# Filler products in parts with fixed places, and attention heads as a pipeline of groups, in a two-layer hybrid decoder step on one core

## The chip, the cores and the metric

The program runs on one core of one Trainium2 chip. The time is the device time of one execution in microseconds (us). The kernel before was timed in three runs; the numbers of stages come from one further execution taken with a profile.

## The reference

One inference step of a decoder with two layers, for a prompt of 1024 tokens and for 8 sample tokens with a paged cache of 512 earlier positions each. The model width is 1024, the MLP width 4096, all in 32-bit floats.

```python
# layer 0                                   # layer 1
h = rmsnorm(x)                              h = rmsnorm(x)
a = diff_attention(h)   # 4 heads, T5 bias  a = forgetting_attention(h)  # 8 heads
b = hgrn2(h)            # 4 heads, scan     b = mlstm(h)                 # 4 heads, scan
x = x + concat(a, b) @ w_out                x = x + concat(a, b) @ w_out
x = x + relu(rmsnorm(x) @ w_up)**2 @ w_down # the same in layer 1, then a final rmsnorm
# differential attention, causal:
p = softmax(q1 @ k1.T / 8 + bias) - lam * softmax(q2 @ k2.T / 8 + bias)
# forgetting attention, causal, F the running sum of log forget values:
p = softmax(q @ k.T / 8 + F_q - F_k);  out = p @ v
```

New key and value rows, states and the normed outputs are returned.

## The kernel before

**Products.** A 32-bit product is computed as three products of values split into a high and a low part (`mm3`, L115): high by high, high by low, low by high. Weights come in blocks of 128 x 1024, loaded by SP's queue, rounded by ScalarE (L100) and subtracted by GpSimd (L101). The tokens are in two halves, u = 0 with 512 columns and u = 1 with 520, the latter as two blocks of 260 (`BLOCKS`). A unit of projection or of the MLP's up step is 24 products, a unit of the down step 12 (L121), each closed by VectorE.

**Heads.** In `diff_head` (L645) and `fox_head` (L1192) the queries of a half are four blocks of 128, taken as two groups g of two blocks. For each block: score products (`scores`, L557), the minimum on VectorE, the exponential on ScalarE (L587), the scaling (L669 and L670, or L1211 and L1213). Then, for each pair j of key blocks, the probabilities are transposed by TensorE (`prob_t`, L605), copied and split by ScalarE and VectorE (`split_t`, L593 and L594), and multiplied with the values (`pv`, L621). `pv` needs both halves of the split. A head's output goes through DRAM (`os`).

**Filler.** While the heads and the scans run, other work is given to TensorE by generators: `fill` holds projections of layer 0 and the halves of the MLP (`half`, L1303), `back` the sample work. `tick(n)` (L165) adds rate x n to a credit and takes one unit for each whole credit; a generator that says "wait" stops it. The heads tick after each score by L / 1024, L being the number of keys. `half` computes first the output projection of the scan's heads, then that of the attention heads, then an RMS (L240 to L254), then eight chunks of four up and eight down units. In layer 0 it says "wait" before its last down units, until the next stage has made room.

**Order.** The stages follow in `run` (L1440): gates and projections, first HGRN half (0.55 units per tick), first differential half (2.6), second differential half (1.5), second HGRN half with the layer's sample work (0.8); then for each u the rest of the filler, the odd projections, the forgetting half (5.0 for u = 0, 1.9 for u = 1), the mLSTM half (1.7, 1.0); at the end the last MLP half alone. The filler of u = 0 is the second half of layer 0's MLP, that of u = 1 the first half of layer 1's.

The order of the text isn't yet that of the engines' queues. The program is built with

```python
    with tile.TileContext(nc, schedule_with_timeline_sim=True) as tc:
```

so that a planner walks its own model of time and gives each engine the earliest instruction of the text that the model holds ready. An engine executes its queue in the order that results. Two accumulators in PSUM (`accM`) serve the filler.

## Time and profile before

| | us |
|---|---|
| median of three runs (2909.43 to 2916.26) | 2913.05 |
| the profiled execution | 2911.51 |
| its span, from the first to the last instruction | 2909.8 |
| mean granted TensorE clock | 0.961 of full speed |

The profile gives for each engine its busy time, and for each stretch of time the busy times, the number of instructions (x), the granted clock of TensorE as a share of 2.4 GHz, the busy share of the DMA engines and their rate. A product's recorded duration (0.28 us for 260 columns, 0.40 for 512) is longer than the distance at which products follow each other, since they overlap.

### The profile page before, as it was taken

The page shows a single profiled execution, that of the slowest core. Times are in us where ns is not written, and L with a number is a line of the kernel's source. Part 1 is how long each engine was busy: PE and PEld are TensorE (multiplying, and loading weights), DVE is VectorE, ACT ScalarE, POOL GpSimd, SP SyncE. Part 2 cuts the span into 40 slices and gives each one's busy share as a digit, 9 for nine tenths or more (in the row PEclk, how much of TensorE's full clock was granted, in tenths as well). Part 3 has the DMA queues.
Part 4 walks back from the last instruction along what each step waited for, and adds up shares of the span by engine and source line. Part 5 has one row for each costly group of instructions (what it writes and reads, how often), then busy time and mean ns, then how long its engine had stood idle before and what let it go on. Part 6 is the DMA issues. An engine that isn't in the chain of part 4 may idle for free. (4 is left out here: it accounts for less than half of the span.)

```text
span 2909.8 us, 44551 instructions
## 1 busy us (share of the span) xinstructions
PE 2772.4 (95%) x17408; PEld 2462.5 (85%) x17410; DVE 1357.5 (47%) x2668; ACT 1037.1 (36%) x1741; POOL 1147.6 (39%) x688
## 2 busy tenths in 40 slices
PE   8999997999999989989999989989999997999997
PEld 6999886888777768889999979978888875999997
DVE  5134468554456654374322255364444354522224
ACT  4111356454212312374332332154444331423233
POOL 3323323443338424432343435843433330344443
PEclk9999998999989979999999999999999995999998
DMA  4332544333436544533322254643322365322222
GB/s 143 113 121 81 157 143 130 103 93 105 146 87 193 170 146 146 163 89 107 123 87 91 92 156 152 226 126 95 93 91 79 98 173 156 95 89 94 94 88 74
DMA packets 174684, 349.72 MB, mean 120 GB/s; under 512 B 28914, under 2 KB 67298, under 8 KB 174474
## 3 DMA queue, kind: packets, MB, share of 16 engines
q1 hardware_dynamic: 174250, 346.81, 38.0%
q8 instruction: 137, 2.24, 0.3%
q0 software_dynamic: 224, 0.07, 0.2%
q14 instruction: 73, 0.60, 0.1%
HBM read 297.92 MB, written 48.88 MB: 119 GB/s over the span
## 5 line engine op out<-in xcount | busy, mean ns | idle before, releaser
L101 POOL TENSOR_TENSOR wl<-wr,wh 128x1024 fp32r<-128x1024 f32 (+1 forms) x361 | 870.2, 2411 | 1306.9 <-ACT wh L100 1221.3
L100 ACT ACTIVATE wh<-wr 128x1024 fp32r<-128x1024 f32 (+1 forms) x361 | 381.4, 1057 | 1038.9 <-PE acc L121 746.7
L121 PE MATMUL acc<-uh,wh 128*128 128x260 f32 (+1 forms) x2080 | 670.4, 326 | 33.1 <-DVE x L1324 15.6
L121 PE MATMUL acc<-ul,wh 128*128 128x260 f32 (+1 forms) x2080 | 663.8, 320 | 0.6 <-DVE ul L1292 0.3
L121 PE MATMUL acc<-xh,wh 128*128 128x260 f32 (+1 forms) x1760 | 588.6, 335 | 12.9 <-ACT xh L217 7.8
L121 PE MATMUL acc<-uh,wl 128*128 128x260 f32 (+1 forms) x1856 | 600.0, 324 | 0.0
L121 PE MATMUL acc<-xl,wh 128*128 128x260 f32 (+1 forms) x1760 | 585.9, 333 | 2.9 <-DVE xl L218 2.9
L121 PE MATMUL acc<-xh,wl 128*128 128x260 f32 (+1 forms) x1760 | 582.8, 331 | 0.0
L121 PEld LDWEIGHTS acc<-uh,wh 128*128 128x128 f32 x2080 | 393.7, 191 | 68.0 <-DVE x L1324 20.8
L121 PEld LDWEIGHTS acc<-ul,wh 128*128 128x128 f32 x2080 | 395.8, 190 | 29.9 <-DVE ul L1292 2.0
L1324 DVE TENSOR_TENSOR x<-acc,x 128x260 f32<-128x260 f32 (+1 forms) x464 | 237.4, 516 | 382.8 <-PE acc L121 382.0
L121 PEld LDWEIGHTS acc<-uh,wl 128*128 128x128 f32 x1856 | 352.7, 190 | 26.9 <-issue 0.2
L121 PEld LDWEIGHTS acc<-xh,wh 128*128 128x128 f32 x1760 | 332.6, 189 | 47.7 <-ACT xh L217 8.1
L121 PEld LDWEIGHTS acc<-xl,wh 128*128 128x128 f32 x1760 | 333.8, 190 | 32.3 <-DVE xl L218 3.9
L121 PEld LDWEIGHTS acc<-xh,wl 128*128 128x128 f32 x1760 | 333.3, 189 | 31.6 <-issue 1.3
L1298 DVE SCALAR_TENSOR_TENSOR acc<-acc,rb 128x260 f32<-128x260 f32 (+1 forms) x192 | 100.1, 523 | 236.8 <-PE acc L121 232.5
L121 PE MATMUL acc<-ih,wh 128*128 128x260 f32 (+2 forms) x600 | 192.3, 321 | 5.6 <-ACT wh L100 2.7
L121 PE MATMUL acc<-ih,wl 128*128 128x260 f32 (+2 forms) x600 | 190.5, 320 | 3.9 <-POOL wl L101 3.8
L121 PE MATMUL acc<-il,wh 128*128 128x260 f32 (+2 forms) x600 | 191.2, 319 | 0.0
L194 DVE TENSOR_TENSOR z<-acc,rb 128x512 f32<-128x512 f32 (+1 forms) x138 | 69.5, 510 | 249.5 <-PE acc L121 224.3
L1301 DVE TENSOR_TENSOR ul<-acc,uh 128x260 fp32r<-128x260 f32 (+1 forms) x192 | 98.5, 514 | 162.8 <-ACT uh L1300 162.3
L121 PE MATMUL acc<-x,wh 128*128 128x260 f32 x448 | 127.9, 288 | 0.8 <-DVE z L194 0.6
(406 smaller groups left out, 3884.1 us busy)
## 6 DMA issues: line engine op xcount, KB each, us to landing
wr<-in_w_up SPq DMA_DIRECT2D x128, 512.0 KB
wr<-in_w_down SPq DMA_DIRECT2D x128, 512.0 KB
wr<-in_w_in_o SPq DMA_DIRECT2D x48, 512.0 KB
wr<-in_w_out SPq DMA_DIRECT2D x32, 512.0 KB
wr<-in_w_in_e SPq DMA_DIRECT2D x27, 512.0 KB
qd<-qS SPq DMA_DIRECT2D x64, 128.0 KB
dk<-in_cache_k_a SPq DMA_DIRECT2D x32, 256.0 KB
dk<-in_cache_v_a SPq DMA_DIRECT2D x32, 256.0 KB
```

The source lines that it names most:

```text
L100: nc.scalar.activation(h[:, :kk, :m], r[:, :kk, :m], AF.Copy)
L101: nc.gpsimd.tensor_tensor(l[:, :kk, :m], r[:, :kk, :m], raw(h[:, :kk, :m]), op=ALU.subtract)
L121: nc.tensor.matmul(out, lhsT=w[:, k, :m], rhs=a[:, sl], start=(n == 0), stop=(n == last))
L194: nc.vector.tensor_tensor(d, p, r, op=ALU.mult)
L1298: nc.vector.scalar_tensor_tensor(p, p, 0.0, self.rb[u][:, sl], op0=ALU.max, op1=ALU.mult)
L1301: nc.vector.tensor_tensor(L[:, sl], p, raw(H[:, sl]), op=ALU.subtract)
L1324: nc.vector.tensor_tensor(x[f][:, sl], pt[:, :m], x[f][:, sl], op=ALU.add)
```

## The change

- `mm3_parts` splits a unit into parts of up to 4608 columns: a unit of 24 products of 512 columns becomes three parts of 8, one of 12 becomes two of 6. The generators give back a part's size in units of 4096 columns, and `tick` takes parts while the credit is above zero.
- While heads run (`self.chain`), the first product of each part is ordered behind the head product that was traced last (`self.after`): a score, a transpose or a `pv` product. The tie holds for TensorE's queue order.
- `attend` runs the heads as a pipeline of groups. In the first halves the scores stand two groups ahead, in the second halves one; loads stand up to one group further ahead. Between the transposes of a pair and its `pv` products come a tick and a share of the next group's score steps. Values are loaded and split a head ahead, and the heads' ends tick too.
- `pv` takes all terms of the high part before those of the low part.
- The rates are changed to parts. In the heads the rate is 1.

```diff
+    def mm3_parts(self, out, h, l, ah, al, ks, sl, m=128):
...
+        todo = [(w, a, k) for k in ks for w, a in ((h, ah[k]), (h, al[k]), (l, ah[k]))]
+        last = len(todo) - 1
+        per = -(-len(todo) // -(-len(todo) * cols // 4608))
+        for i in range(0, last + 1, per):
+            if i:
+                yield per * cols / 4096
+            for n in range(i, min(i + per, last + 1)):
+                w, a, k = todo[n]
+                with self.tc.issue_after(self.after) if self.chain and self.after and n == i else nullcontext():
+                    nc.tensor.matmul(out, lhsT=w[:, k, :m], rhs=a[:, sl], start=(n == 0), stop=(n == last))
+        return (last + 1 - i) * cols / 4096
...
-            while credit >= 1 and gens:
+            while credit > 0 and gens:
                 try:
-                    if next(gens[0]) == "wait":
+                    size = next(gens[0])
+                    if size == "wait":
+                        credit = 0.0
                         break
-                    credit -= 1
+                    credit -= size or 1
                 except StopIteration:
                     gens.pop(0)
...
-            nc.tensor.matmul(S[:, cs], lhsT=q2[:, qs], rhs=k2[:, cs], start=False, stop=True)
...
+
...
+        self.chain = True
+        N = len(groups)
+        for G in groups[:depth + lead]:
+            G.prep()
+        self.tick(4)
+        for G in groups[:depth]:
+            for step in G.steps:
+                step()
+                self.tick(0.7)
+        for n, G in enumerate(groups):
+            if n + depth + lead < N:
+                groups[n + depth + lead].prep()
+            nxt = groups[n + depth] if n + depth < N else None
+            todo = list(nxt.steps) if nxt else []
+            for j in range(G.pairs):
+                parts = G.tr(j)
+                share = 0 if nxt and nxt.late and j < G.pairs - 2 else -(-len(todo) // (G.pairs - j if not (nxt and nxt.late) else min(2, G.pairs - j)))
+                self.tick(max(gap - 0.4 * share, 0.4))
+                for _ in range(share):
+                    todo.pop(0)()
+                G.pv(j, parts)
+            G.end()
+        self.chain = False
...
                     n += 128
...
-            order = [(k0, t) for t in terms(k0)] + [(k1, t) for t in terms(k1)]
-        else:
-            t0 = terms(k0)
-            order = [(k0, t0[0])] + [(k1, t) for t in terms(k1)] + [(k0, t) for t in t0[1:]]
+        order = []
+        for x in range(2):
+            t0, t1 = ([(kb, t) for t in terms(kb) if t[1] == x] for kb in (k0, k1))
+            order += t0[:1] + t1 + t0[1:] if x == 0 else t1 + t0
         for n, (kb, (w, x)) in enumerate(order):
             half = kb == 2 * g + 1
...
+        def prep(h, g):
             if g == 2 * u:
...
+                if need:
+                    self.drain("fill", need[h])
+                parts[h] = self.diff_parts(h, u, hd)
+                if h == 0:
+                    vt[0] = self.values(self.O["va"][0:128, :], u, hd)
+
+        def score(h, i, m):
+            S = pS.tile([128, W], F32, name="S", tag="S")
+            L = self.scores(S, parts[h][m], i)
+            w = min(L, 256)
+            if m == 0:
+                st[h, i] = hd.tile([128, 2, 2], F32, name="st", tag="st", bufs=8)
+            es[m] = hd.tile([128, W], F32, name="e", tag="e", bufs=5 if u else 7)
+            self.soft_neg(S, L, es[m], st[h, i][:, m, :], self.bias[:, h, 256 - w:])
+            if m == 0:
...
+            P[h, i] = es[0]
+
+        def tr(h, g, j):
+            if h == j == 0 and g == 2 * u:
+                V[0] = self.diff_values(vt[0], u, hd, pm)
+            if g == 2 * u and j == 0:
+                po[h] = pm.tile([128, 512], F32, name="po", tag="po", bufs=1)
+                if h < 3 and not need:
+                    vt[h + 1] = self.values(self.O["va"][128 * h + 128:128 * h + 256, :], u, hd)
+            return self.prob_t(hd, pm, (P[h, 2 * g], P[h, 2 * g + 1]), g, j)
+
+        def pv(h, g, j, p):
+            Vh, Vl = V[h]
+            self.pv(po[h][:, 256 * (g % 2):256 * (g % 2) + 256], g, j, p, lambda kb: ((Vh[:, kb, :], 0), (Vh[:, kb, :], 1), (Vl[:, kb, :], 0)))
+
+        def end(h, g):
+            if g == 2 * u:
+                if h < 3:
+                    if need:
+                        vt[h + 1] = self.values(self.O["va"][128 * h + 128:128 * h + 256, :], u, hd)
+                    V[h + 1] = self.diff_values(vt[h + 1], u, hd, pm)
+                return
+            ot = hd.tile([128, 512], F32, name="ho", tag="ho", bufs=1)
+            self.head_norm(hd, po[h][:], pm, ot[:], self.lc[:, 6:7], None, 512, eps=self.lc[:, 4:5], thr=self.lc[:, 5:6])
+            nc.sync.dma_start(self.os[0][u][h][:, :512], ot[:])
+            self.tick(2.5 if u else 1.5)
+
+        groups = []
+        for h in range(4):
...
+                steps = [lambda h=h, i=i, m=m: score(h, i, m) for i in (2 * g, 2 * g + 1) for m in range(2)]
+                groups.append(Group(lambda h=h, g=g: prep(h, g), steps, g + 1, lambda j, h=h, g=g: tr(h, g, j),
+                                    lambda j, p, h=h, g=g: pv(h, g, j, p), lambda h=h, g=g: end(h, g), late=u == 1 and g == 2))
+        self.attend(groups, 1 if u else 2, 0 if u else 1, 1.3 if u else 1.0)
...
-                self.fill = (0.55, hp + dp)
+                self.fill = (1.1, hp + dp)
...
-                self.fill = (2.6, self.fill[1] + [self.half(0, 0, accM, accM)])
+                self.fill = (1, self.fill[1] + [self.half(0, 0, accM, accM)])
...
             self.heads_done.add((0, 0))
-            self.fill = (1.5, self.fill[1])
...
-                self.fill = (0.8, self.fill[1])
+                self.fill = (1.6, self.fill[1])
                 self.back = (1.1, [self.hgrn_sample(ph, pm, pS), self.diff_sample(ph, pm, pS)])
...
-                    self.fill = (0, [self.half(u, 1 - u, accM, accM)])
-                    for _ in range(8):
-                        next(self.fill[1][0])
+                    self.fill = (1, [self.half(u, 1 - u, accM, accM)])
+                    self.tick((6, 12)[u])
+                    self.fill = (0, self.fill[1])
...
-                            self.back = (1, [self.fox_keys(ph, pm)])
-                        for _ in self.fox_project(ph, ps, j, u) if j < 12 else self.mlstm_project(ph, ps, j, u):
-                            self.tick()
+                            self.back = (0.7, [self.fox_keys(ph, pm)])
...
-                self.fill = ((5.0, 1.9)[u], self.fill[1])
+                self.fill = (1, self.fill[1])
...
-                self.fill = ((1.7, 1.0)[u], self.fill[1])
+                self.fill = ((1.7, 2.0)[u], self.fill[1])
```

`fox_half` is rewritten in the same manner: two score steps per group, values once for two heads, `self.attend(groups, 1 if u else 2, 1, 1.3 if u else 1.0)`, a tick of 0.8 for each block of four value transposes and for each head's end. The first halves hold 7 (differential) and 6 (forgetting) `e` buffers, the values of the differential heads 2.

## Rows read from the trace of the kernel before

**Rows 1.** The page, engines' busy time with share of the span and number of instructions.
```profile
PE 2772.4 (95%) x17408; PEld 2462.5 (85%) x17410; DVE 1357.5 (47%) x2668; ACT 1037.1 (36%) x1741; POOL 1147.6 (39%) x688
```

**Rows 2.** The table by stretches of 50 us: the stretch, its length, the busy time and instructions of TensorE, weight loads, VectorE, ScalarE, GpSimd; the granted clock; the DMA share; GB/s.
```profile
400.00:450.00 50.00, 45.11 (x242) 37.88 (x241) 37.63 (x80) 28.30 (x59) 17.64 (x8) 0.96 0.61 188
450.00:500.00 50.00, 37.79 (x154) 29.80 (x153) 41.75 (x69) 31.22 (x51) 16.67 (x6) 0.84 0.41 116
500.00:550.00 50.00, 50.00 (x240) 42.46 (x240) 29.39 (x57) 26.87 (x42) 15.63 (x9) 0.93 0.21 64
...
650.00:700.00 50.00, 50.00 (x249) 41.62 (x248) 27.06 (x49) 25.10 (x38) 15.82 (x8) 1.00 0.23 74
...
1200.00:1250.00 50.00, 45.77 (x306) 41.43 (x306) 30.73 (x58) 28.50 (x57) 25.49 (x17) 1.00 0.52 159
1250.00:1300.00 50.00, 45.45 (x347) 43.75 (x346) 35.50 (x89) 34.39 (x88) 15.26 (x10) 0.93 0.32 95
...
1650.00:1700.00 50.00, 44.45 (x362) 43.42 (x361) 27.42 (x47) 24.09 (x41) 19.32 (x9) 1.00 0.48 148
1700.00:1750.00 50.00, 44.62 (x255) 38.39 (x256) 23.25 (x33) 12.71 (x18) 15.08 (x8) 0.93 0.45 137
...
1900.00:1950.00 50.00, 40.37 (x195) 33.01 (x193) 37.63 (x57) 28.72 (x49) 19.68 (x11) 0.90 0.39 109
```

**Rows 3.** The same table for other stretches.
```profile
460.00:765.00 305.00, 296.70 (x1414) 245.45 (x1415) 177.69 (x305) 155.41 (x240) 115.87 (x49) 0.97 0.32 97
1275.00:1325.00 50.00, 50.00 (x417) 49.61 (x416) 33.51 (x85) 35.36 (x87) 15.88 (x8) 1.00 0.28 87
1890.00:2325.00 435.00, 423.47 (x2086) 353.02 (x2085) 202.99 (x311) 203.96 (x317) 169.27 (x74) 0.99 0.32 97
1008.00:1050.00 42.00, 23.11 (x49) 12.64 (x50) 27.12 (x69) 4.91 (x10) 4.97 (x7) 0.55 0.77 242
2398.50:2472.50 74.00, 57.34 (x235) 41.97 (x235) 36.06 (x126) 10.16 (x28) 6.17 (x13) 0.52 0.52 160
...
2325.00:2398.50 73.50, 72.67 (x342) 53.29 (x342) 42.57 (x104) 26.03 (x49) 29.07 (x35) 0.98 0.61 168
775.00:985.00 210.00, 202.46 (x990) 162.81 (x988) 117.74 (x217) 50.74 (x74) 119.20 (x90) 0.92 0.50 146
```

**Rows 4.** The table by stretches for line 121 alone, the weight products of `mm3`: busy time and number of products, of weight loads; clock; DMA.
```profile
460.00:765.00 305.00, 240.89 (x969) 179.08 (x970) 0.97 0.32 97
1275.00:1325.00 50.00, 34.41 (x265) 32.44 (x264) 1.00 0.28 87
1890.00:2325.00 435.00, 355.71 (x1446) 265.33 (x1445) 0.99 0.32 97
1008.00:1050.00 42.00, 5.68 (x20) 4.80 (x20) 0.55 0.77 242
2398.50:2472.50 74.00, 3.78 (x17) 3.78 (x18) 0.52 0.52 160
```

**Rows 5.** The timeline of TensorE: start in us, duration, line, product and number. The first two rows are the first and the last of 18 products that follow each other without a break; the last two are a pair of the mLSTM stage at two places.
```profile
1001.73 0.39 PE L121 MATMUL acc<-uh,wh 128*128 128x512 f32 x1
...
1005.67 0.39 PE L121 MATMUL acc<-uh,wl 128*128 128x512 f32 x1
...
2396.15 0.49 PE L1045 MATMUL pm<-mvr,mP 128*128 128x129 f32 x2
...
2419.93 0.80 PE L1045 MATMUL pm<-mvr,mP 128*128 128x129 f32 x2
```

**Rows 6.** Who TensorE waited for from 985 to 1053: us in total, times, longest.
```profile
PE pm L765 <- DVE ov L767: 13.4, 8, 2.7
```

**Rows 7.** Groups of instructions by line and shape over the span: number, busy us, mean ns of one, idle time before them.
```profile
L1324 DVE TENSOR_TENSOR x<-acc,x 128x512 f32<-128x512 f32 x160 | 109.5, 687 | 136.1 <-PE acc L121 135.5
...
L594 DVE TENSOR_TENSOR Pl<-pm,Ph 128x512 fp32r<-128x512 f32 x72 | 49.5, 687 | 50.4 <-ACT Ph L593 49.6 <-ACT rb L256 0.7
...
L1298 DVE SCALAR_TENSOR_TENSOR acc<-acc,rb 128x512 f32<-128x512 f32 x64 | 44.6, 697 | 96.6 <-PE acc L121 93.6 <-ACT rb L256 2.9
L1301 DVE TENSOR_TENSOR ul<-acc,uh 128x512 fp32r<-128x512 f32 x64 | 44.0, 688 | 60.4 <-ACT uh L1300 60.4
...
L593 ACT ACTIVATE Ph<-pm 128x512 fp32r<-128x512 f32 x72 | 42.7, 594 | 64.1 <-PE pm L605 63.7
```

**Rows 8.** Who TensorE waited for from 425 to 500 (first two rows) and from 500 to 765 (the last).
```profile
PE po L621 <- DVE Pl L594: 5.4, 3, 2.7
PE S L565 <- ACT e L587: 5.0, 3, 2.8
...
PE po L621 <- DVE Pl L594: 1.2, 1, 1.2
```

**Rows 9.** The table by stretches for line 605 alone, the transposes of `prob_t`.
```profile
1275.00:1325.00 50.00, 7.34 (x43) 5.04 (x43) 1.00 0.28 87
```

More of the change, by code (lines that the diff above doesn't have):

```diff
@@ L1 @@
 import math
-from contextlib import ExitStack
+from contextlib import ExitStack, nullcontext
 import numpy as np
@@ L55, in tile, with __init__ @@
         return pool.tile(shape, dt, name=name, tag=tag or name, **kw)
+class Group:
+    def __init__(self, prep, steps, pairs, tr, pv, end, late=False):
+        self.prep, self.steps, self.pairs, self.tr, self.pv, self.end, self.late = prep, steps, pairs, tr, pv, end, late
 class Step:
@@ L113, in first_block, with mm3 @@
         return h, l
-    def mm3(self, out, h, l, ah, al, ks, sl, m=128):
+    def mm3(self, *a):
+        self.now(self.mm3_parts(*a))
+    def mm3_parts(self, out, h, l, ah, al, ks, sl, m=128):
         nc = self.nc
-        n, last = 0, 3 * len(ks) - 1
-        for k in ks:
-            for w, a in ((h, ah[k]), (h, al[k]), (l, ah[k])):
-                nc.tensor.matmul(out, lhsT=w[:, k, :m], rhs=a[:, sl], start=(n == 0), stop=(n == last))
-                n += 1
+        cols = sl.stop - sl.start
+        todo = [(w, a, k) for k in ks for w, a in ((h, ah[k]), (h, al[k]), (l, ah[k]))]
[9 more added lines that the diff above has]
+        return (last + 1 - i) * cols / 4096
     def project(self, ps, src, evict, us=(0, 1), m=128, w=None):
@@ L154, in project_to @@
         for u in us:
-            for _ in self.project(ps, None, ev, (u,), w=(h, l)):
-                yield
+            yield from self.project(ps, None, ev, (u,), w=(h, l))
             nc.sync.dma_start(dst(u), z[:, HS[u].start - t0:HS[u].stop - t0])
@@ L567, in scores, with attend @@
                 nc.tensor.matmul(S[:, L - 128:L], lhsT=self.idr[:], rhs=self.tri[:], start=False, stop=False)
-            nc.tensor.matmul(S[:, cs], lhsT=q2[:, qs], rhs=k2[:, cs], start=False, stop=True)
+            self.after = nc.tensor.matmul(S[:, cs], lhsT=q2[:, qs], rhs=k2[:, cs], start=False, stop=True).ins
         return L
+    def attend(self, groups, depth, lead, gap):
+        self.chain = True
[21 more added lines that the diff above has]
+        self.chain = False
     def softmax(self, sm, S, L, e, st):
@@ L604, in prob_t @@
                 if kb <= 2 * g + r:
-                    nc.tensor.transpose(pt[:, n:n + 128], P[r][:, 128 * kb:128 * kb + 128], self.ident[:])
+                    self.after = nc.tensor.transpose(pt[:, n:n + 128], P[r][:, 128 * kb:128 * kb + 128], self.ident[:]).ins
                     n += 128
@@ L620, in pv @@
             c = 256 * (kb - k0)
-            nc.tensor.matmul(o[:, 128:] if half else o, lhsT=w, rhs=parts[x][:, c:c + (128 if half else 256)],
-                             start=(j == 0 and n == 0), stop=(j == g and n == len(order) - 1))
+            self.after = nc.tensor.matmul(o[:, 128:] if half else o, lhsT=w, rhs=parts[x][:, c:c + (128 if half else 256)],
+                                          start=(j == 0 and n == 0), stop=(j == g and n == len(order) - 1)).ins
     def diff_parts(self, h, u, hd):
@@ L1355, in half @@
                     pt = acc()
-                    self.mm3(pt[:, :m], h, l, xh, xl, range(KC), slice(o, o + m))
+                    size = yield from self.mm3_parts(pt[:, :m], h, l, xh, xl, range(KC), slice(o, o + m))
                     if alone and cc == f == 0:
```

184 lines of the change are left out of this document (83 added, 101 removed).

## The prediction

> **What bounds the kernel now.** I read the page first. The span is 2909.8 us, the profiled execution took 2911.51 us, and the three timed runs have a median of 2913.05 us. TensorE is busy for 2772 us, 95% of the span; no other engine passes 47% [rows 1]. The sum of TensorE's products is therefore the floor, and only stretches in which it idles, or runs at the lower of its two clock levels, can be won. The change leaves out no product.
>
> So I went on to the table by stretches. For each stretch I count as lost its length minus busy time times granted clock, since a product at 1.2 GHz takes about twice as long as at 2.4: the same pair of L1045 products runs for 0.49 us in one place and 0.80 in the other [rows 5]. In the dense stretch 650 to 700 nothing is lost [rows 2]. Five places lose:
> - 1008 to 1050: 42 - 23.11 x 0.55 = 29 us [rows 3]. This is the end of the sample work behind the second HGRN half.
> - 2398.5 to 2472.5: 74 - 57.34 x 0.52 = 44 us [rows 3]. This is the end of the second mLSTM half with its samples.
> - The turn from the first differential half to the second, 400 to 550: 6.7 + 18.3 + 3.5 = 28.5 us. The start of the first forgetting half, 1200 to 1300: 4.2 + 7.7 = 12 us. The start of the second, 1900 to 1950: 13.7 us [rows 2].
> - 775 to 985, the second HGRN half: 210 - 202.46 x 0.92 = 24 us, most of it by the clock [rows 3].
> - 1650 to 1750: 5.6 + 8.5 = 14 us, where a filler half ends in its RMS and nothing stands beside it [rows 2].
>
> The first two have one cause: the filler has run out. Only 20 and 17 weight products stand in them [rows 4], the last one of the half ends near 1005.7 [rows 5], and TensorE then waits for VectorE's L767 (13.4 us in 8 waits) [rows 6].
>
> Where did the filler go? Products of 512 columns follow each other every (1005.67 - 1001.73) / 17 = 0.232 us [rows 5]. The first filler half, from its heads' part to the place where it says "wait", has 96 + 768 + 672 = 1536 such products (356 us); the third has 1728 (401 us). The second differential half swallows 969 of the first (225 us), the second forgetting half 1446 of the third (335 us) [rows 4]. The ticks in the old text ask for less: in the latter a head's four scores give 3.25, times 8 heads and the rate 1.9 that is 49 units of 12 or 24 products, 16 on average, 183 us. The planner took the rest early, because it fills every hole it sees with the next ready product. What is eaten there is missing at 1008 and at 2398.
>
> **The change, part by part.** A part is 8 products of 512 columns, 8 x 0.232 = 1.86 us.
>
> Rates outside the heads: 0.55 to 1.1, 0.8 to 1.6, 1.0 to 2.0 are the old rates in new units (a unit of 24 or 12 products is 3 or 1.5 parts, 2.0 on average), so the pace there is the old one. In the odd projections 0.7 per part replaces 1 per unit of 1.5 parts: the same too. Price 0.
>
> Fixed places: the first product of each part is ordered behind the last head product, so in the heads the filler is no more than the ticks ask for. The tie is an order in TensorE's own queue, no semaphore; but TensorE works in order, so behind a head product that waits stand the parts tied to it and every later product. Counting the ticks: the second differential half 48 parts (4 + 2.8 ahead, 1.6 for the first values, 2.3 and 3.6 per pair of groups, 1.6 and 2.5 at the ends), 89 us; the second forgetting half 79 parts, 147 us. So 136 us and 188 us of filler move later. What the later stages ask for: HGRN with samples 48 x 1.6 + 27 x 1.6 = 120 parts, after 46 of 192: 26 parts are left over. mLSTM with samples 28 x 2 + 7 x 2 = 70, after 12 + 79 of 216: 55 are left and are drained densely. Both starved stretches then have filler: minus 29 and minus 44 us (bounds: nothing, and both whole).
>
> The heads with less filler. Own TensorE work of the second differential half: 296.7 x 0.97 - 225 = 63 us, of the second forgetting half 423.5 x 0.99 - 335 = 84 us [rows 3, 4]. With the new filler they need 152 and 231 us instead of 305 and 435. VectorE must keep up. A chunk of 192 filler products (44.5 us) costs it 4 x (0.697 + 0.688) + 8 x 0.687 = 11.0 us [rows 7]. So of 177.7 us there [rows 3], 5.05 x 11 = 56 are the filler's; it will need 122 + 22 = 144 us in 152. In the forgetting half, by the same count (203.0 - 83 + 36), it needs 156 in 231. The first is at 95%, and its products will wait for VectorE: I take 18 us. The second is loose, 7 us. Together plus 25 us. Each of the 28 + 56 key-block pairs carries transposes, then L593 and L594 (0.594 + 0.687 us) [rows 7], then products that need both; in between stand a tick of 0.5 to 1.3 parts (0.9 to 2.4 us) and a score step, which cover it. Bounds: zero, as at 1275 to 1325, where 265 products of 260 columns gave a thinner filler and nothing was idle [rows 3, 4]; and 84 x 1.8 = 151 us, if every pair pays the 5.4 us in 3 waits that the unfilled turn shows [rows 8]. The value is nearer the first row, since the filler's share is the same.
>
> Pipelining: the scores of the next group stand between the transposes of this one, values are loaded and split a head ahead, and waits of that kind at the starts (S on e, 5.0 us, Pl 5.4 us) [rows 8] should shrink. But a good part of these starts is the filler's own RMS (L240 to L254) and its gains on VectorE, which stay. I take a third of 54: minus 19 us (bounds 0 and 40). The loads issue the same DMAs on SP's queue, a head earlier; behind them only weight loads queue, which are some parts ahead. Price 0.
>
> What is late next: the third half now ends in dense work, and its closing RMS stands bare before the last half, which needs its buffers. The place at 1650 to 1750 is the nearest row: plus 14 us (0 to 20). It was hidden in the starved stretch.
>
> Finer parts in HGRN: lumps of 24 products become 8, so the small products stand between filler more evenly; of the 24 us I take 4 (0 to 20). The refilled stretches keep some loss, as the filled sample work at 2325 to 2398 does (73.5 - 72.67 x 0.98 = 2.3, 3%) [rows 3], over some 200 us: plus 6. Net plus 2.
>
> Sum: -29 - 44 - 19 + 25 + 14 + 2 = -51 us, from 2911.5 to 2860.5; the median of the runs lies 1.5 us above the profiled execution, so 2862 us.
>
> **The rivals.**
> - *Everything closes.* The heads lose nothing, the starts give 40, HGRN 20: -29 - 44 - 40 - 20 + 14 = -119, 2794 us. For it: the empty idle column of 1275 to 1325. Against: VectorE at 95%.
> - *The places don't hold.* Only the first product of a part is tied, and only while heads run; filler that is traced later (HGRN, mLSTM) is free, and the planner may pull it into the holes of the heads as it did before. Then the starved stretches stay: about 2909 us. Against: the free parts come behind tied ones in the same accumulators.
> - *VectorE takes TensorE's place.* In the heads nothing may now fill a late Pl, and TensorE works in order. Without the 25 us the gain is 76 us; over 84 pairs the change is slower from 0.9 us per pair on. At 1.8 us [rows 8] it costs 151: 2988 us. For it: the 95%. Against: 500 to 765 shows a single wait of this kind, 1.2 us [rows 8], though under 2.5 times the filler.
> - *The clock falls in the heads.* 450 to 500, where filler was thin, ran at 0.84 [rows 2]. Over 383 us of heads that is 16%, 61 us: 2923 us. Against: with 43 transposes in 50 us and the share of filler that the change leaves, 1275 to 1325 kept 1.00 [rows 3, 9]. The Trainium skill, "TensorE: Matmul & The Clock Gate", section "A second HAM failure mode: psum-queue depth-cycling", describes this case: products that cycle through PSUM buffers leave TensorE idle briefly but often between groups, and the clock swings between its levels. By that rule the time is this rival's 2923 us, by the row of 1275 to 1325 the forecast's 2862; the turn at 450 agrees with the rule, the later row doesn't, and no row shows this mixture with a single transpose buffer and so little filler.
>
> **How the numbers follow.** Chances: my forecast 0.48, everything closes 0.17, places don't hold 0.12, VectorE 0.16, the clock 0.07. A measurement of this kernel tells about 0.2% (6 us) from no change. Faster by more than that: the first two, 0.65, and a part of the rest (0.07), 0.72. Within: 0.08, most of the third. Slower: 0.20. The forecast's own range, from its bounds, is 2830 to 2895. For 8 in 10 I go from 2800 to 2925, which leaves out most of VectorE's case and the far end of the first rival.
>
> **What would show it.** Right: weight products all through the stretches that correspond to 1008 and 2398, at clock 1.0; the second differential and forgetting halves at about 170 and 240 us, with some 390 and 630 weight products; a dense stretch behind mLSTM and an RMS bare at its end. Wrong: 900 and 1400 weight products in these halves again (places don't hold); L621 waiting for L594 all through them, or L605 for L670 (VectorE); a granted clock under 0.95 there (clock). The forecast as a whole is wrong if the starved stretches are filled and the time is still above 2895.

## The result, and the profile after

The changed kernel takes 2947.75 us (median of 4 runs, 2941.49 to 2948.05) against 2913.99 us (4 runs, 2909.43 to 2916.26): a ratio of 1.0113, 95% interval 1.0094 to 1.0131. It is slower by 34 us, where 51 us less were forecast, and lies outside the range. The profiled execution took 2948.05 us, its span is 2946.3 us at a mean granted clock of 0.970 (before 0.961).

On the page of the changed kernel TensorE is busy as long as before (2772.6 to 2772.4 us [rows 1]). Summed over the span, the difference is therefore idle time; by stages, idle time and clock both move, and partly cancel:

```profile
PE 2772.6 (94%) x17410; PEld 2458.7 (83%) x17410; DVE 1375.5 (47%) x2668; ACT 1039.1 (35%) x1741; POOL 1141.5 (39%) x688
```

The table by stretches, cut at the stages. The columns are those of [rows 2]: stretch, length, busy time and instructions of TensorE, weight loads, VectorE, ScalarE, GpSimd; granted clock; DMA share; GB/s. First the kernel before: first and second differential half, second HGRN half with its samples, first and second forgetting half, second mLSTM half with its samples.

```profile
335.00:453.00 118.00, 113.11 (x662) 97.03 (x661) 77.05 (x198) 62.31 (x141) 39.57 (x31) 0.97 0.56 175
453.00:776.00 323.00, 310.57 (x1476) 255.88 (x1475) 187.75 (x322) 159.62 (x246) 121.21 (x53) 0.97 0.34 103
776.00:1055.00 279.00, 251.87 (x1170) 197.65 (x1171) 166.60 (x319) 68.62 (x103) 132.10 (x101) 0.87 0.53 159
...
1222.00:1338.00 116.00, 106.97 (x828) 102.40 (x829) 86.78 (x198) 78.56 (x185) 38.98 (x25) 0.97 0.37 112
...
1901.00:2328.00 427.00, 415.47 (x2043) 345.41 (x2042) 198.05 (x311) 197.37 (x307) 163.77 (x78) 0.99 0.30 93
2328.00:2461.00 133.00, 122.19 (x547) 89.31 (x548) 75.12 (x223) 33.81 (x71) 33.24 (x37) 0.76 0.59 171
```

The same six stages of the changed kernel:

```profile
328.00:463.00 135.00, 121.61 (x687) 102.86 (x688) 74.08 (x198) 63.84 (x145) 40.80 (x33) 0.92 0.50 156
463.00:682.00 219.00, 188.61 (x906) 153.37 (x905) 149.78 (x276) 123.32 (x201) 62.05 (x30) 0.93 0.31 95
682.00:1069.00 387.00, 361.38 (x1726) 291.77 (x1727) 201.74 (x360) 104.87 (x146) 189.69 (x126) 0.97 0.46 140
...
1234.00:1347.00 113.00, 101.14 (x738) 95.19 (x736) 87.40 (x193) 80.11 (x189) 34.03 (x24) 0.94 0.38 106
...
1935.00:2202.00 267.00, 243.01 (x1252) 202.51 (x1251) 157.93 (x245) 143.99 (x242) 83.78 (x46) 0.95 0.29 86
2202.00:2389.00 187.00, 185.49 (x898) 140.32 (x898) 96.14 (x232) 52.50 (x92) 65.58 (x49) 0.98 0.48 135
```

The starved stretches are gone: mLSTM with samples now runs at a clock of 0.98 instead of 0.76, HGRN at 0.97 instead of 0.87. The four head stages went the other way. TensorE's idle time there, length minus busy, is 4.9 + 12.4 + 9.0 + 11.5 = 38 us before and 13.4 + 30.4 + 11.9 + 24.0 = 80 us after, and the clock fell from 0.97, 0.97, 0.97, 0.99 to 0.92, 0.93, 0.94, 0.95.

The same table for the weight products alone (line 121 before, line 141 after; busy time and number), second differential half, HGRN, second forgetting half, mLSTM. Before:

```profile
453.00:776.00 323.00, 251.85 (x1015) 187.44 (x1014) 0.97 0.34 103
776.00:1055.00 279.00, 167.32 (x645) 125.19 (x646) 0.87 0.53 159
1901.00:2328.00 427.00, 346.94 (x1408) 258.57 (x1408) 0.99 0.30 93
2328.00:2461.00 133.00, 45.59 (x176) 33.15 (x176) 0.76 0.59 171
```

After:

```profile
463.00:682.00 219.00, 119.95 (x445) 85.58 (x444) 0.93 0.31 95
682.00:1069.00 387.00, 299.68 (x1201) 226.56 (x1202) 0.97 0.46 140
1935.00:2202.00 267.00, 164.28 (x618) 114.23 (x617) 0.95 0.29 86
2202.00:2389.00 187.00, 136.77 (x541) 99.14 (x542) 0.98 0.48 135
```

The filler did move about as the ticks ask: 1015 products became 445 in one head stage, 1408 became 618 in the other. To compare stages with different amounts I take a stage's **remainder**: its length less its weight products at their dense pace, 0.232 us for 512 columns [rows 5], 0.119 for 260 (in the timeline of TensorE, start and duration first, the second row is ten products behind the first and 1.19 us later):

```profile
2699.84 0.28 PE L141 MATMUL acc<-xh,wl 128*128 128x260 f32 x1
...
2701.03 0.28 PE L141 MATMUL acc<-xh,wh 128*128 128x260 f32 x1
```

The remainder holds the stage's own products and all that is lost, and since both kernels have the same products, the differences of the remainders add up to the difference of the spans. In us, from the counts by shape and the exact ends of the stages (the last half ends with TensorE's last product; some 9 us follow it in both kernels):

| stage | products before, after | remainder before, after | difference |
|---|---|---|---|
| up to the first head | 1676, 1620 | 70.8, 73.0 | +2.2 |
| first differential half | 454, 480 | 40.2, 55.0 | +14.8 |
| second differential half | 1014, 444 | 87.3, 115.5 | +28.2 |
| HGRN and samples | 648, 1200 | 134.7, 108.6 | -26.1 |
| first odd projections | 792, 756 | 4.2, 7.8 | +3.6 |
| first forgetting half | 516, 420 | 54.6, 62.8 | +8.2 |
| first mLSTM half | 516, 444 | 27.9, 29.1 | +1.2 |
| second odd projections | 3528, 3762 | 37.5, 43.6 | +6.1 |
| second forgetting half | 1408, 618 | 101.1, 124.5 | +23.4 |
| mLSTM and samples | 176, 540 | 91.7, 61.0 | -30.7 |
| last half | 3456, 3900 | 28.0, 34.0 | +6.0 |

The filled stages give 57 us, the heads take 75, all else 19: +37, the difference of the spans (36.5). Each number comes from one profile. Kernels that have the same order of products up to a stage's end show how well a stage repeats: the first differential half has remainders of 55, 51 and 54 us in three of them, HGRN differs by some 7 us (last section).

Who TensorE waited for (us in total, times, longest), in the second differential half of the changed kernel:

```profile
PE S L586 <- ACT e L636: 9.3, 11, 3.4
PE pm L654 <- DVE Vl L695: 8.1, 3, 3.3
PE acc L261 <- DVE sq L251: 3.4, 1, 3.4
PE pm L654 <- DVE e L727: 3.2, 1, 3.2
PE po L669 <- DVE Pl L643: 2.6, 3, 1.2
PE po L669 <- ACT Ph L642: 2.1, 3, 0.7
```

In its second forgetting half:

```profile
PE S L586 <- ACT e L636: 6.8, 4, 4.4
PE pm L654 <- DVE VV L1268: 6.2, 4, 1.9
...
PE po L669 <- DVE Pl L643: 3.7, 5, 1.2
PE po L669 <- ACT Ph L642: 1.9, 2, 1.4
```

In the same halves of the kernel before, the first row being of the differential one, the others of the forgetting one:

```profile
PE S L565 <- ACT e L587: 5.0, 3, 2.8
...
PE pm L605 <- DVE VV L1189: 6.5, 1, 6.5
...
PE S L565 <- ACT e L587: 1.2, 2, 0.9
```

The long ones are not the chain Ph, Pl that I had feared for every pair (4.7 us in the first of these halves, as before, and 5.6 in the second, before 0.7), but buffers: a score product that waits for the exp (L636) to free a score buffer, and a transpose that waits until VectorE has read the split values (Vl, VV) out of the buffer that it shares with them. The two kinds have 17.4 of 30.4 us of idle time in the first of these halves (before 5.0 of 12.4) and 13.0 of 24.0 in the second (before 7.7 of 11.5). VectorE as a whole is not the bound: it is busy for 149.8 us of 219 and 157.9 of 267.

### The profile page after: what moved, and what is told of

Read it like the earlier page. It is cut to its first block, busy times and chain, and to the rows that moved or that the text cites. A ratio compares the mean times of both kernels' runs of the same rounds, so it can differ in the third digit from the quotient of the medians.

```text
span 2946.3 us, 44581 instructions
## 1 busy us (share of the span) xinstructions
PE 2772.6 (94%) x17410; PEld 2458.7 (83%) x17410; DVE 1375.5 (47%) x2668; ACT 1039.1 (35%) x1741; POOL 1141.5 (39%) x688
## 3 DMA queue, kind: packets, MB, share of 16 engines
q1 hardware_dynamic: 174250, 346.81, 37.5%
## 5 line engine op out<-in xcount | busy, mean ns | idle before, releaser
L1431 DVE TENSOR_TENSOR x<-acc,x 128x260 f32<-128x260 f32 (+1 forms) x464 | 238.0, 517 | 402.7 <-PE acc L141 400.8
```

Of the source, the lines that this page charges most:

```text
L1431: nc.vector.tensor_tensor(x[f][:, sl], pt[:, :m], x[f][:, sl], op=ALU.add)
```

## The experiments

Three theories stood for the 75 us. **Places**: the ties keep the planner from putting filler where a product waits. **Thin filler**: with less than half the filler beside each pair, the waits come bare wherever it stands. **Pipeline**: scoring ahead holds the score buffers. Each run was timed beside the kernel before on the same chip; ratios are to that, and differences between runs timed apart are taken from the ratios. The remainders below are of the second differential half (D), HGRN (H), the second forgetting half (F) and mLSTM (M), with the number of weight products.

**No ties.**
```diff
-                with self.tc.issue_after(self.after) if self.chain and self.after and n == i else nullcontext():
+                with self.tc.issue_after(self.after) if False else nullcontext():
```


> The changed kernel without its fixed places: the parts are still yielded where the heads call for them, but nothing ties a part behind the instruction recorded last, so the planner may move them. Three theories for the 75 us that the head stages lost against the kernel before (changed kernel 2948, before 2914). Theory places (the ties keep the planner from putting filler where a product waits): the loss goes, 2880 to 2900 us, and the idle time of TensorE in the two second halves falls from 70 us together to under 40. Theory thin filler (less than half of the old filler lies beside each pair, so waits on the exp and on VectorE come bare whatever the order): 2940 to 2955, no change over 10 us. Theory pipeline (running the next group's scores ahead holds the score buffers and lengthens the waits on them): 2940 to 2955 too.

2928.35 us, 1.005 (1.0028 to 1.0073): 18 us less than the changed kernel, between the forecasts. But the amount changed with the ties. The weight products alone, in D and F:

```profile
466.00:774.00 308.00, 232.96 (x924) 172.97 (x924) 0.95 0.33 100
...
1917.00:2352.00 435.00, 352.89 (x1424) 262.12 (x1424) 0.98 0.30 94
```

924 and 1424, nearly as before: the planner took the later filler forward again. D falls to 93.7, F to 104.7, and H and M rise again to 120.7 and 94.8. So the ties are what holds filler back, and the run can't tell places from amount.

**Old heads, no ties.** `diff_head`, `fox_head` and their callers as before, parts and all else as changed, rates 5.0, 1.9, 2.7, 3.0 per L / 1024 in the four head stages, ties off.
```diff
-        self.attend(groups, 1 if u else 2, 0 if u else 1, 1.3 if u else 1.0)
+        parts = nxt(0)
+        for h in range(4):
+            parts = self.diff_head(h, u, hd, pm, pS, parts, lambda: nxt(h + 1))
...
-                self.fill = (1, self.fill[1])
+                self.fill = ((2.7, 3.0)[u], self.fill[1])
```


> The heads of the kernel before (one head after the other, scores and softmax of a block pair, then its products), with the parts of 4096 columns, without ties, and with rates set so that each head stage issues about as many weight products as in the changed kernel (about 390 in the second differential half, 620 in the second forgetting half); all else as in the changed kernel. Theory pipeline: the old order with as little filler loses nothing, 2860 to 2890 us. Theory thin filler: it loses as much as the pipeline or more, 2935 to 3000, since the old order has each pair's waits bare too. Theory places: 2870 to 2900, as there are no ties here.

2910.83 us, 0.9993 (0.9971 to 1.0016). The filler wasn't thin: 918 products in D and 1408 in F. What it does show is that the finer parts cost nothing that can be told from noise.

**More filler at the fixed places.**
```diff
             self.heads_done.add((0, 0))
+            self.fill = (1.5, self.fill[1])
...
-                self.fill = (1, self.fill[1])
+                self.fill = ((1, 1.5)[u], self.fill[1])
```


> The changed kernel with half as much filler again in the second half of the differential heads and in that of the forgetting heads (rate 1 to 1.5 there, nothing else). Theory thin filler: each of the about 84 pairs of the two second halves gets back 0.3 to 0.4 us of hidden waiting and the waits fall, 2915 to 2930 us, unless the starved stretches behind come back. Theory places: within 8 us of 2948, as the parts lie at the same fixed places. Theory pipeline: within 8 us of 2948.

2925.35 us, 1.0024 (1.0003 to 1.0045), as thin filler expected: 26 us less. D falls from 115.5 at 444 products to 95.8 at 598, F from 124.5 at 618 to 117.5 at 912, and H stays (108.0). Not every wait shrinks: in D the transposes wait for Vl 0.8 us instead of 8.1, but the scores for the exp 9.3 us as before. The products come from where they hid nothing: 444 weight products stood between the mLSTM stage and the last half, 324 of them are now gone from there.

**Old heads with ties.** As the old heads above, ties on.
```diff
+        self.chain = True
         for h in range(4):
             parts = self.diff_head(h, u, hd, pm, pS, parts, lambda: nxt(h + 1))
+        self.chain = False
```


> As the run with the old heads and thin filler, but with the ties on inside the heads: each part stands right behind the score product, transpose or value product that was recorded last. What it costs beside that run is the price of the ties alone under the old order. Theory places: 30 to 75 us over that run. Theory thin filler and theory pipeline: within 10 us of it.

2991.29 us, 1.0264 (1.0219 to 1.0310): 80 us over the run without ties. I had written that this would speak for places. But here the filler is thin (744 and 852 products), so again two things changed. What can be compared is the order at fixed places: F takes 155.8 at 852 products in the old order, 117.5 at 912 in the pipeline; D 113.5 at 744 against 95.8 at 598. The pipeline hides waits that the old order has bare. That is against the theory pipeline. The order of TensorE's products in the trace shows it too: in F, 15 of the 56 pairs have no weight product between their transposes and their value products, in the pipeline with as much filler 2 (in the kernel before 1, in the changed kernel 3).

**Loose ties.** A part is tied to the last product ahead of its group (or head), not to the one recorded last: free inside the group, not ahead of it.
```diff
-                with self.tc.issue_after(self.after) if self.chain and self.after and n == i else nullcontext():
+                with self.tc.issue_after(self.floor) if self.chain and self.floor and n == i else nullcontext():
...
         for n, G in enumerate(groups):
+            self.floor = self.after
```


> The changed kernel with its ties loosened: a part is tied behind the last product before its group of two query blocks, not behind the product recorded last, so the planner may move it freely inside the group but not into an earlier one. The run without any ties left open whether places or thin filler cost the heads, since the planner took the filler of later stages forward and the second differential half had its old 300 us of length back; here it can't. Theory places: the head stages lose less with as few products beside them (about 900 in the two differential halves, 620 in the second forgetting half), 2890 to 2920 us. Theory thin filler: as few products hide as little wherever they stand, 2935 to 2955.

2993.39 us, 1.0298 (1.0261 to 1.0335): 54 us worse than the changed kernel, where places expected 30 to 60 less. The row of all engines for F:

```profile
1939.00:2254.00 315.00, 274.02 (x1289) 221.49 (x1287) 167.68 (x249) 147.04 (x244) 86.71 (x47) 0.89 0.25 75
```

F takes 164.7 us at 646 products. Its longest waits are these two, the second one seldom seen in the changed kernel:

```profile
PE S L586 <- ACT e L637: 15.2, 15, 5.3
PE po L670 <- ACT Ph L643: 12.3, 17, 1.4
```

Free filler is used up at the first waits of a group, and the later pairs stand bare: 29 of F's 56 pairs have no weight product between transposes and value products, where the changed kernel has 3. Places fall: at this amount the fixed places are worth 54 us.

> The same loosened ties with half as much filler again in the two second halves. The run with that filler at fixed places took 2925. Theory places: 10 to 30 us below that, 2895 to 2915. Theory thin filler: within 8 us of 2925.

With rates 1.5 and loose ties: 2949.08 us, 1.0129 (1.0096 to 1.0162). Again more filler gives time back (44 us), and again fixed places are better (by 31 us).

> The heads of the kernel before with thin filler, as in the run with ties on the old heads (2991 us), but each part tied only behind the last product before its head. Theory places: most of the 80 us between the old heads with ties (2991) and without (2911) goes, 2900 to 2930 us, with the filler still as thin. Theory thin filler: 2960 to 2995. If it lies clearly below the pipeline with the same loose ties, the pipeline itself costs time.

Old heads with loose ties: 2975.97 us, 1.0221 (1.0185 to 1.0257). It lies only 13 us below the old heads with fixed places, so most of the 80 us between the old heads with and without ties came with the amount. The 13 are not the price of the places alone, since the amount differs again (636 and 712 products for 744 and 852). The run lies 17 us below the pipeline with loose ties, but that one has 492 and 646 products. At like amounts F is as long in both (165.7 to 164.7), and D is 10 us better in the old order (106.8 at 636, 116.4 at 660 in the run before this). The pipeline's gain needs the fixed places.

**The same filler, split over the pair.**
```diff
-                self.tick(max(gap - 0.4 * share, 0.4))
+                slot = max(gap - 0.4 * share, 0.4) / (share + 1)
+                self.tick(slot)
                 for _ in range(share):
                     todo.pop(0)()
+                    self.tick(slot)
```


> The changed kernel with the same amount of filler per pair, but split over the pair: a share of it ahead of each score step and one ahead of the value products, in place of all of it behind the transposes. Theory places: waits for the exp of the score steps fall, and the time by 10 to 40 us (or it rises by as much, if the evictions behind the transposes now come bare). Theory thin filler: within 8 us of 2948.

2961.24 us, 1.0173 (1.0139 to 1.0207), 17 us worse: F rises to 136.7, D to 122.7 at unchanged amounts. Of F's 56 pairs 10 are now bare between transposes and value products, for 3. The place behind the transposes is the better one.

**Filler by the stage tables.**
```diff
+            self.fill = (1.9, self.fill[1])
...
-                self.fill = (1.6, self.fill[1])
+                self.fill = (1.5, self.fill[1])
...
-                self.fill = (1, self.fill[1])
+                self.fill = ((1, 1.9)[u], self.fill[1])
```


> The changed kernel with its fixed places and more filler, set from the stage tables of the runs so far: rate 1.9 in the two second halves of heads (1 before) and 1.5 in the second HGRN stage (1.6). About 740 weight products should then lie in the second differential half (444 in the changed kernel, 598 in the run with half as much again) and 1150 in the second forgetting half (618, 912), taken from the 444 that the changed kernel sends behind everything and from the HGRN stage, which the other runs show full with 890. Theory thin filler: the second differential half loses about 90 us beside its weight products (115 in the changed kernel, 87 in the one before), the forgetting one about 108 (124, 100), nothing comes back in the stages behind, and the time is 2890 to 2915 us. Rival, that the amount no longer matters and fixed places are the cost: 2918 to 2930, as with rate 1.5.

2911.33 us, 0.999 (0.9968 to 1.0012). The whole loss is won back by the amount. D takes 93.3 at 780 products, M 66.9, H 89.6; F only falls to 115.3 at 1152. What stays there is mostly one kind of wait, 16.0 of 20.7 us of idle time:

```profile
PE pm L654 <- DVE VV L1268: 16.0, 4, 8.2
```

The 8.2 us end 28 us into F. From 1919.4 to 1928.0, ahead of that split of the values, VectorE is for more than half of the time at the filler's own steps (L1431, L239, L251). And one term comes back: the last half's remainder rises from 34.0 to 39.7, since no filler is left ahead of it.

**Old order in the first halves.** As that run, with `diff_head` and `fox_head` of before and no ties in the first halves, and with rates of 5.0 and 2.7 per L / 1024 there, which give about the same amounts (468 and 430 products for 481 and 432).
```diff
-                self.diff_half(0, hd, pm, pS, dp[2::3])
+                self.diff_half0(0, hd, pm, pS, dp[2::3])
...
-                    self.fox_half(u, hd, pm, pS)
+                    (self.fox_half if u else self.fox_half0)(u, hd, pm, pS)
```


> The run with the higher rates, with the heads of the first halves (first differential and first forgetting half) as in the kernel before and without ties; the second halves keep the pipeline and the fixed places. The first differential half lost 15 us more than before in the changed kernel with as many weight products beside it (480 against 454), so thin filler can't be its cause. Theory start (the pipeline of depth two loads and scores three groups before its first value products, with only four parts to fill that): 15 to 25 us below the run with the higher rates, 2868 to 2895. Rival, that the first half pays for the finer parts: within 6 us of it.

2898.09 us, 0.9951 (0.9922 to 0.9980): faster than both kernels, 13 us below the run before, a little less than the 15 to 25 expected. The first halves take 46.1 + 56.3 us instead of 54.0 + 62.8. In front of the last half TensorE now shows one wait:

```profile
PE acc L141 <- ACT uh L1531: 17.7, 1, 17.7
```

**Filler beside the bias products.** In `diff_consts`:
```diff
             nc.sync.dma_start(self.bd[h], bt[:])
+            self.tick(1)
```


> The run with the higher rates with one part of filler after each of the four bias products that stand ahead of the first differential half; in the changed kernel TensorE waits there for GpSimd and ScalarE with nothing beside it, and runs at a mean granted clock of 0.74 in that stretch (325 to 350 us). Theory start: 5 to 12 us below the run with the higher rates. Rival (the stretch is bound by the loads of the first keys, not by filler): within 3 us of it.

2910.22 us, 0.9995 (0.9973 to 1.0018), 1 us below: the time that the rival gave. That the loads of the keys bind the stretch is not shown by it. The first differential half stays at 54.5.

**Filler held back.** As the run with the old order in the first halves, less for F and M.
```diff
-                self.fill = ((2.7, 1.9)[u], self.fill[1])
+                self.fill = ((2.7, 1.7)[u], self.fill[1])
...
-                self.fill = ((1.7, 2.0)[u], self.fill[1])
+                self.fill = ((1.7, 1.6)[u], self.fill[1])
```


> The run with the old order in the first halves and the higher rates (2898), with some filler held back for the junction ahead of the last half: rate 1.7 instead of 1.9 in the second forgetting half and 1.6 instead of 2.0 in the second mLSTM stage. In that run TensorE waits 17.7 us in one piece for the first product of the last half (the kernel before 6.4, the changed kernel, with 444 products of filler left over, nothing). Theory junction (the bare normalisation ahead of the last half, a term of the prediction, is back as soon as the filler is used up): about 100 to 150 products lie there, the wait falls below 3 us, the forgetting half and the mLSTM stage lose 3 to 6 us more, and the time is 2885 to 2896. Rival (the wait is for a load or an order, not for lack of filler): the wait stays, 2898 to 2906.

2891.26 us, 0.9927 (0.9900 to 0.9953), the lowest time of all; the interval overlaps that of the run that it builds on. 92 products now stand ahead of the last half, the 17.7 us wait is gone (the longest there is 3.9 us), its remainder falls from 39.2 to 31.3, F and M stay (116.4, 65.8). So that wait was lack of filler.

**Pipeline one group deep in the first halves.** Ties on, the higher rates.
```diff
-        self.attend(groups, 1 if u else 2, 1, 1.3 if u else 1.0)
+        self.attend(groups, 1, 1, 1.3 if u else 1.0)
```


> The run with the higher rates (2911), with the pipeline one group deep instead of two in both first halves, fixed places as they are. The first halves lost 20 us more with the pipeline than with the old order. Theory start: scoring two groups ahead before any value product is what they pay for; with one, half or more of it goes, 2896 to 2905 us, and TensorE idles less than 10 us in the first differential half (16 in that run). Rival places (the ties inside the first halves are the cost, as the run with the old order there was without ties): within 4 us of 2911.

2915.09 us, 1.0011 (0.9989 to 1.0033): no gain. The first differential half keeps its idle time (13.7 us) and its clock:

```profile
331.00:464.00 133.00, 119.33 (x675) 101.73 (x675) 76.90 (x198) 63.67 (x144) 38.28 (x32) 0.92 0.50 158
```

The theory start falls with it and with the run with filler beside the bias products. What is left: with about 440 to 530 products that half takes 52.8 in the pipeline without ties, 53.6 in the old order with ties, 51 to 55 in six profiles with both, and 40 to 46 with neither. Either alone costs as much as both; why isn't settled.

**The old amount at fixed places.** As the run with the old order in the first halves, more for F.
```diff
-                self.fill = ((2.7, 1.9)[u], self.fill[1])
+                self.fill = ((2.7, 2.45)[u], self.fill[1])
```


> The run with the old order in the first halves and the higher rates, with the rate of the second forgetting half at 2.45 instead of 1.9, so that about as many weight products lie there at fixed places (1400 to 1480) as without ties (1424) or in the kernel before (1408). The mLSTM stage behind it is then starved as it was, so the time says little; what counts is what that half takes beside its weight products (0.232 us each): 100 us in the kernel before, 104 in the pipeline without ties, 115 with ties and 1152 products. Theory amount: 98 to 106 us. Theory places (beyond some 900 products more filler doesn't reach the waits at fixed places): 111 to 117.

2914.10 us, 1.0006 (0.9982 to 1.0030); M is starved again (101.1 at 87 products). F:

```profile
1888.00:2343.00 455.00, 368.29 (x1497) 276.98 (x1497) 0.98 0.31 92
```

455 - 1497 x 0.232 = 107.7, with the exact ends 106.8: just above what the amount theory gave and below the range for places. At fixed places F runs 124.5, 117.5, 116.4, 115.3, 106.8 with 618, 912, 1043, 1152, 1497 products. Of the 23 us that it lost, 18 are the amount; 6 stay, of which the pipeline without ties has 4 (104.7). But only 9 of the 18 come back while M is still filled.

## Why the prediction was wrong

- *The filler moves, and the starved stretches fill*: right, and close in number. 445 products for some 390 forecast, 618 for 630, 444 left over behind mLSTM for 55 x 8 = 440. The two stages gave 57 us for the 73: HGRN 26 for 29 and mLSTM 31 for 44. By the prediction's own measure (length minus busy time times clock) the filled mLSTM stage loses the 3% that was left to it (187 - 185.49 x 0.98 = 5 us), HGRN 9% (387 - 361.38 x 0.97 = 36 us).
- *The heads with less filler, +25 (18 and 7), and pipelining, -19*: this step failed. Together +6 was forecast (a third of 54 is 18, not 19), and the four head stages cost +75. For the second halves alone it is +52 where 25 was taken and the bounds were 0 and 151; the 18 us of it that stood for a VectorE at 95% had the wrong cause. So the fault is the value taken: I took the end at 1275 to 1325 [rows 3, 4] as the nearer row "since the filler's share is the same". It is a cut of 50 us, without a loss, of the first forgetting half, which as a whole idles 9.0 of 116 us at a clock of 0.97. And in that half a block's scores reach 512 keys and, by the pool sizes in the code, there are three score buffers and two for transposes; the second halves have up to 1024 keys, two and one. Of the waits that came, the larger part is of just these buffers. That the buffers make the difference between the halves is argued from the wait rows; no run had more of them, since the second halves' pools leave no room. That the thin filler is what the second halves pay for is shown by the remainders: D comes back fully (95.8 at 598 products, where the untied kernels have 87 to 98 at 900 and more), F from 124.5 to 115.3 at 1152 and to 106.8 at 1497, with 101.1 before. The waits need not shrink one by one: in F those of the scores fall (6.8 us to 1.6 at 1152), those of the transposes for VV grow (6.2 to 16.0).
- *Pipelining as such* is worth something, but only where filler is thin: F 38 us at about 900 products and fixed places. In the two runs without ties, at 920 and 1400 products, pipeline and old order are level (D 94 to 97, F 105 to 103). In the first halves, which were hardly thinned (454 to 480 and 516 to 420 products), it saved nothing: they lost 15 and 8 us, where the prediction had only a gain at their starts. So 23 of the 75 us are not the amount's; they come with the pipeline or the ties, and the cause stays open.
- *VectorE takes TensorE's place*: the direction of this rival came, not its cause. VectorE needed 150 and 158 us (144 and 156 forecast), but in 219 and 267 us, not in 152 and 231. The loss per pair in the second halves is 52 / 84 = 0.6 us, below the 0.9 that the rival needed; it decided because 57 us less the 19 elsewhere left only 38 to eat. In one place VectorE did set the pace, at the start of F with more filler (8.2 us, above).
- *The clock falls in the heads*: about a quarter of the loss. By the prediction's measure a clock below 1 by d costs d of the busy time: 113.1 x 0.03 + 310.6 x 0.03 + 107.0 x 0.03 + 415.5 x 0.01 = 20 us before, 121.6 x 0.08 + 188.6 x 0.07 + 101.1 x 0.06 + 243.0 x 0.05 = 41 after. So by this estimate 42 us of the 75 are idle time and 21 the clock; 12 are neither. The measure takes a product to last twice as long at half the clock; the pair in [rows 5] took 1.6 times as long (0.80 us for 0.49). The rival had put 0.84 and 61 us; its sign, a clock under 0.95, came in the second differential half (0.93) and at its edge in the second forgetting half (0.95). The Trainium skill, "TensorE: Matmul & The Clock Gate", section "A second HAM failure mode: psum-queue depth-cycling", tells of a kernel in which short, frequent idling between groups of products, as it cycles through PSUM, makes the clock go back and forth; these stages (0.92 to 0.95, no wait over 4.4 us) agree.
- *The bare RMS ahead of the last half, +14*: not in the changed kernel, whose left-over filler covers it, but real: 17.7 us as soon as the filler is used up, gone with 92 products held back. The stages besides heads and starved ones cost 19 us all the same, spread over five of them (2.2, 3.6, 1.2, 6.1, 6.0) for which the forecast had nothing; that this is near its 14 + 2 is luck.
- *Finer parts*: free, as far as the old heads without ties can tell (0.9993).
- *The places don't hold*: they hold. Without them the starved stretches come back.

So the change is slower because it moves more filler out of the heads than the stages behind can use: 444 products hid nothing ahead of the last half. Put back, they undo the loss (0.999). With the old order, untied, in the first halves and some filler held back for the junction, the pipeline and the fixed places in the second halves make 2891 us, 0.9927 of the kernel before.

## What to carry to other kernels

Filler is one pool: before an order holds it back from one stage, count what the stages behind will take, and keep what would be left over where it was. A price for "less cover" is read from a row with the same buffers and the same sizes, not only the same share of filler. And a run that lifts an order may change the amount too; look at the counts by stage before its time is given a meaning. Where filler is thin, count the pairs that have none between a product and the one that waits for its result: a fixed place behind each transpose left 3 of 56 bare, free placing within a group 29.

## What was unexpected of the hardware

A stage's time does not quite repeat. Three of the kernels (those with the old order in the first halves alone) have the same order of TensorE's products up to the second forgetting half. Their HGRN stage took 294 us at a clock of 0.98, 301 us at 0.96 and 295 us at 0.98:

```profile
729.00:1023.00 294.00, 281.00 (x1382) 226.79 (x1382) 173.36 (x332) 79.81 (x116) 155.87 (x112) 0.98 0.53 160
...
728.00:1029.00 301.00, 281.45 (x1380) 227.53 (x1378) 180.25 (x331) 79.10 (x115) 154.67 (x111) 0.96 0.51 157
...
728.00:1023.00 295.00, 281.46 (x1381) 226.65 (x1380) 173.09 (x331) 79.44 (x116) 155.59 (x111) 0.98 0.52 158
```

TensorE is busy as long in all three; what differs is idle time and the clock. The second differential half ahead of it repeats within 0.3 us (remainders of 93.9 to 94.2). A difference of some 7 us in the HGRN stage between two single profiles says nothing, and the 26 us that it gained in the table are good to about that; no verdict here rests on H.
